# First pair's first five token tiles in float32r pairs beside the conditioning, the residual gate's row in four pieces, and u's loads in another order

## The chip, the core and the metric

The kernel runs on one core of a Trainium2 chip. The metric is the time of one execution on the device in microseconds (us): the median of three runs before the change is 989.02 us (987.64 to 989.61). The core's engines work side by side, each through its own queue in order: TensorE (PE; its weight loads are listed as PEld), VectorE (DVE), ScalarE (ACT), GpSimd (POOL), and SyncE (SP), which here only issues DMA transfers.

## The reference, cut to what matters

One layer works on 1,152 tokens: 1,024 samples (8 tiles of 128) and 128 prompt tokens (tile 8), D_MODEL = 1024, everything in float32.

```python
shift, scale, gate = split(silu(cond) @ w_ada + b_ada, 3)      # conditioning, one row per kind of token
h = rmsnorm(x, norm_g) * (1 + scale) + shift
q, k, v, z_a, u_b, z_b, u_c, z_c, g_a, g_b, g_c = split(h @ w_in)
q = rmsnorm(heads(q), q_g); k = rmsnorm(heads(k), k_g)
y_a = attention(q, k, v)          # window of 8 x 16 and 128 cached keys
y_b = real(fft2(u_b)) @ w_fnet    # Fourier mixing
y_c = pool(u_c) * pool_scale      # centred means over 2, 4, 8, 16 tokens
merged = sigmoid(g_a)*((silu(z_a)*y_a) @ p_a) + sigmoid(g_b)*((silu(z_b)*y_b) @ p_b) + sigmoid(g_c)*((silu(z_c)*y_c) @ p_c)
y = x + gate * (merged @ w_o)     # also returned: k and v of the prompt
```

## The kernel before, in words

Float32 products are made of pairs: an operand is split into a high part and the rest, and `mm3` (lines 163 to 166) issues three matmuls, high by high, high by low and low by high. Pairs are float16 with a power-of-two scale in the projections (`split16`, line 111), and float32r without a scale in the later small products (`two`, `split_r`). A float32r matmul of 384 columns counts as one instruction, as a float16 one does; a plain float32 matmul is two.

**Start (lines 331 to 558, in the order written out by hand, each engine in the order of the program).** The conditioning needs the 8 MB of `w_ada`'s shift and scale parts. `load_wa` brings 16 pieces of 512 KB into 6 buffers; `ada_piece` (line 390) multiplies a piece, two plain float32 matmuls in 32-column groups of the array (`tile_position`), and after every four pieces `ada_row` copies the row out (ACT) and `ada_end` transposes it (PE) and forms a quarter of `gs` and `sh` (DVE). Between them the nine x tiles go through `xnorms` (squares on ACT, root on POOL), `xscale` (DVE) and `x_group` (line 379), in three groups of three: for each of 8 column blocks k three transposes into a PSUM bank and one copy into `xT`. When all of `gs` and `sh` is there, `scale_h` (line 421) finds one bound for h and from it `shs`, the power of two by which h becomes float16. Only then can `make_h` (line 455) split h into `hh` and `hl`, and the first projection begins: `p1_mm` for pair 0 (heads 0 and 1: 384 columns of q, k, v), five token tiles at once, block k by block k, 120 matmuls in five PSUM banks (lines 536 to 558). Among these matmuls lie `make_h` of the next k, `head_scales` (line 476), `v_scales` (line 460) and `new_pair` (line 235), the scales that the heads need. `p1_done` (line 269) finishes a tile (squares, roots, norms, float16 pairs), its parts put off by `later` to certain steps; `tick` counts a step. Pair 0's weights come through `prep` (line 115): four loads, four squares on ACT for a scale, a matmul, and four `split16`.

Then a chain of segments fills PE between the attention's steps. Segment 0 is `p1_tiles` of tiles 8, 5, 6, 7 of pair 0 (line 875); among its steps are `prep` of pair 1, `cached_k` and `cached_v`, at step 21 `group_q` (transposes of q, line 636), at step 24 `group_k` and at step 30 `setup_prompt` (line 670).

**Pooling and Fourier stage (lines 1008 to 1246).** Here a planner orders the instructions. `z_chunk` makes the gates z (three chunks of 24 matmuls for each of four row blocks). The u's, written to DRAM by earlier steps, are loaded one after another behind the small constants (lines 1027 to 1050). `pool_sums` and `pool_diff` (DVE) make the centred means, `pool_out` (line 1085) multiplies them chunk by chunk, `gate_chunk` (line 995) gates a chunk: product on DVE, high part on ACT, low part on POOL. The Fourier products follow (`fold`, `over_channels`, `over_positions`), then the gating of branch b in six chunks.

**Branch projections (lines 1249 to 1419, by hand again).** Sixteen steps n of three chunks (18 matmuls of float32r) project branches c and b; `p_next` splits weights two steps ahead (DVE), `p_chunk` copies a chunk out (ACT) and stores it, with six buffers for chunks under way. Beside it `a_load` and `a_gate` bring branch A's y and z and gate them (steps 0 to 11), and `combos` makes sums for a later stage (DVE and ACT). After every second step `add_wg` (line 1352) adds one of eight pieces of the residual gate's row: for each half n a plain float32 matmul into column group m % 4 of a bank; `load_wg` brings 512 KB per piece, two buffers. Steps 16 to 23 project branch A, and the gated merge and the output projection follow; neither is changed.

Of the kernel before, what the change touches and what calls it, by code (L numbers as in the profile page):

```python
# [35 lines left out]
NWA = 6  # L36
# [3 lines left out]
def mixer_layer(ctx: ExitStack, tc: tile.TileContext, xs, xp, smalls, qgrow, kgrow, bgate, wss, wgate, w1, w3, pw, wo,  # L40
# [74 lines left out]
    def prep(pieces, name):  # L115
# [65 lines left out]
    G.memset(mhalf, -0.5)  # L181

# [12 lines left out]
    with tc.tile_pool(name="hp", bufs=1, side="right") as hp:  # L195
        hh, hl = [], []
        for i in range(2):
            hh.append(hp.tile([P, 4, NT], F16, name=f"hh{i}"))
            hl.append(hp.tile([P, 4, NT], F16, name=f"hl{i}"))
# [28 lines left out]
        with tc.tile_pool(name="qkv", bufs=1) as qkv:  # L228
# [40 lines left out]
            def p1_done(c, t, pt, wait):  # L269
# [61 lines left out]
            with tc.tile_pool(name="st", bufs=1) as st:  # L331
# [12 lines left out]
                def load_x(t):  # L344
                    xt[t] = st.tile([P, D], F32, tag="xt", name=f"xt{t}", bufs=6)
                    nc.sync.dma_start(xt[t], xs[t * P:(t + 1) * P, :] if t < 8 else xp)
# [29 lines left out]
                XG = ((0, 1, 2), (3, 4, 5), (6, 7, 8))  # L376
                xT = st.tile([P, KT, NT], F32, name="xT")

                def x_group(ts):

                    n = len(ts) * P
                    for k in range(KT):
                        pt = bank(("s", "pt", "s")[k % 3], f"xt{k}_{ts[0]}")
                        for i, t in enumerate(ts):
                            T.transpose(pt[:, i * P:(i + 1) * P], xt[t][:, k * P:(k + 1) * P], ident)
                        (V.tensor_copy if k % 2 == 0 else S.copy)(xT[:, k, ts[0] * P:ts[0] * P + n], pt[:, :n])
# [3 lines left out]
                def ada_piece(i):  # L390
                    b, j = divmod(i, 4)
                    if j == 0:
                        pas[b] = bank("p1", f"pa{b}")
# [27 lines left out]
                def scale_h():  # L421
# [5 lines left out]
                    V.scalar_tensor_tensor(ab[:, 3:4], ab[:, 1:2], 31.0, ab[:, 2:3], op0=ALU.mult, op1=ALU.add)  # L427
                    pb = bank("po", "pbd")
# [4 lines left out]
                    V.tensor_scalar(md, ident[:2, :2], m1, None, op0=ALU.mult)  # L433
                    pb2 = bank("po", "pbs")
# [6 lines left out]
                    return hm  # L441

                def v_bound(hm):
# [4 lines left out]
                def h_full(k, eng):  # L448
                    for a, c in ((slice(0, NS), 1), (slice(NS, NT), 0)):
                        if eng is S:  # L450
                            S.activation(xT[:, k, a], xT[:, k, a], AF.Identity, bias=sh[:, k, c:c + 1], scale=gs[:, k, c:c + 1])
                        else:
                            V.tensor_scalar(xT[:, k, a], xT[:, k, a], gs[:, k, c:c + 1], sh[:, k, c:c + 1], op0=ALU.mult, op1=ALU.add)

                def make_h(k):
                    a = slice(0, NT)
                    S.activation(hk(hh, k, a), xT[:, k], AF.Copy, scale=shs)  # L457
                    V.scalar_tensor_tensor(hk(hl, k, a), xT[:, k], shs, hk(hh, k, a), op0=ALU.mult, op1=ALU.subtract)  # L458
# [37 lines left out]
                prep0 = prep_pair(0)  # L496
                wu0 = None
                for what in ("w0", "w1", 0, 1, 2, "w2", "w3", 3, 4, 5, "w4", "w5", "w6", "w7", 6, 7, 8, "w8", "w9", "w10", "w11"):
                    load_x(what) if isinstance(what, int) else load_wa(int(what[1:]))
                run(prep0, 1)  # L500
                for i in range(12, 16):
                    load_wa(i)
# [4 lines left out]
                ada_piece(0)  # L507
                ada_piece(1)
                xnorms(XG[0])
                xscale(XG[0])  # L510
                ada_piece(2)
                ada_piece(3)
                ada_row(0)
                x_group(XG[0])
                ada_end(0)
                xnorms(XG[1])
                xscale(XG[1])
                ada_piece(4)
                ada_piece(5)
                x_group(XG[1])  # L520
                ada_piece(6)
                ada_piece(7)
                ada_row(1)
                xnorms(XG[2])
                ada_end(1)
                ada_piece(8)
                xscale(XG[2])
                x_group(XG[2])
                for i in (9, 10, 11):
                    ada_piece(i)  # L530
                for k in range(4):
                    h_full(k, (S, V)[k % 2])
                ada_row(2)
                ada_end(2)
                run(prep0, 4)
                h_full(4, V)
                h_full(5, V)
                ada_piece(12)
                run(prep0, 1)
                ada_piece(13)  # L540
                run(prep0, 1)
                ada_piece(14)
                run(prep0, 3)
# [9 lines left out]
                for k in range(6):  # L553
# [13 lines left out]
                    if k == 3:  # L567
                        v_scales(vall)
# [1203 lines left out]
```

## Time and profile before

| what | value |
|---|---|
| runs before | 987.64, 989.02, 989.61 us |
| the profiled execution | 992.83 us; span from first to last instruction 990.3 us |
| mean granted TensorE clock | 0.967 |
| busy in the span | PE 922.5, PEld 677.0, DVE 658.8, ACT 489.7, POOL 208.4 us |
| first matmul of pair 0, tile 0 | at 73.89 us |
| first matmul of the branch projections | at 504.96 us |
| moved over the span | 125.02 MB |

The profile is one execution of its own, 3.8 us (0.4%) above the median of the runs. Its page has a strip of 40 slices of 24.8 us: a digit is the busy share of an engine in tenths, PEclk the granted clock in tenths. Rows of the timeline read: start, duration, engine, line, operation, output and inputs, count, and in brackets how long the engine was idle before and what released it. Rows by stretch give for each engine its busy time and, in brackets, its instructions, then the granted clock (1.00 is full), the share of time that the DMA engines were busy, and GB/s. Rows by group give count, total busy us and mean ns of one. SPq is the queue in which SP issues transfers.

### The profile page before, as it was taken

What the parts mean: (1) busy time and instruction counts of PE and PEld (TensorE: products, weight loads), DVE (VectorE), ACT (ScalarE), POOL (GpSimd) and SP (SyncE); (2) the same over time, 40 slices, a digit from 0 to 9 for tenths busy, and PEclk for the clock granted to TensorE, in tenths of its full rate; (3) what the DMA queues carried; (4) which work ended last, traced back from release to release, by engine and by line L of the source; (5) the groups of instructions that cost most, each with busy time, mean ns of one, the idle gap of its engine ahead of it and who ended that gap; (6) DMA issues with size and microseconds to landing.
All of it is one profiled execution on the core that took longest, in us unless ns stands there. A gap on an engine that the chain in (4) does not pass through costs nothing.

```text
span 990.3 us, 17726 instructions
## 1 busy us (share of the span) xinstructions
PE 922.5 (93%) x6554; PEld 677.0 (68%) x6554; DVE 658.8 (67%) x1443; ACT 489.7 (49%) x1017; POOL 208.4 (21%) x352
## 2 busy tenths in 40 slices
PE   4668899999989999998969999999999999999998
PEld 2324566666656666764757779988888888877886
DVE  2347767767767555549767868478989789765322
ACT  3354757757756646644535644545555454442100
POOL 0000765255254332002132200002021020200000
PEclk9568999999999999998988999999999999999999
DMA  7731351251241141250138965453444332228321
GB/s 300 276 107 37 79 152 44 59 170 34 57 131 33 48 149 55 104 188 0 59 104 291 318 237 197 152 176 96 152 126 122 129 105 79 67 71 297 117 75 53
DMA packets 75781, 125.02 MB, mean 126 GB/s; under 512 B 12031, under 2 KB 45227, under 8 KB 75695
## 3 DMA queue, kind: packets, MB, share of 16 engines
q1 hardware_dynamic: 75695, 123.89, 38.8%
q8 instruction: 51, 0.84, 0.3%
q14 instruction: 35, 0.29, 0.1%
HBM read 88.20 MB, written 29.11 MB: 118 GB/s over the span
## 4 chain that ended last, share of the span: by engine, by line
PE 77%; DVE 7%; ACT 5%; DMA 5%; issue 3%; POOL 2%; SPq 1%; ACTq 0%; DVEq 0%; POOLq 0%
PE p L166 3%; PE p L164 3%; PE p L165 3%; PE wo L164 3%; PE wo L166 3%; PE wo L165 3%; PE xc L164 3%; PE xb L164 3%; PE xb L166 3%; PE xc L166 3%; PE xb L165 3%; PE xc L165 3%; PE m L164 3%; PE m L166 3%; PE m L165 3%; PE xa L164 3%
## 5 line engine op out<-in xcount | busy, mean ns | idle before, releaser
L164 PE MATMUL p<-wh_q,hh 128*128 128x384 f16 x288 | 95.3, 331 | 1.9 <-ACT hh L457 1.9
L166 PE MATMUL p<-wh_q,hl 128*128 128x384 f16 x288 | 95.1, 330 | 1.1 <-DVE hl L458 1.1
L165 PE MATMUL p<-wl_q,hh 128*128 128x384 f16 x288 | 95.1, 330 | 0.0
L733 DVE CUSTOM_DVE_ANT_0 sn<-s,bias 128x512 f32<-128x512 f32 x64 | 44.0, 688 | 32.3 <-PE s L729 30.5
L164 PE MATMUL m<-hh,wh_m 128*128 128x384 f16 x192 | 62.6, 326 | 0.0
L166 PE MATMUL m<-hh,wl_m 128*128 128x384 f16 x192 | 62.6, 326 | 0.0
L165 PE MATMUL m<-hl,wh_m 128*128 128x384 f16 x192 | 62.6, 326 | 0.0
L164 PE MATMUL wo<-woh,mh 128*128 128x512 f32 x144 | 56.8, 394 | 1.2 <-ACT woh L1525 1.2
L165 PE MATMUL wo<-wol,mh 128*128 128x512 f32 x144 | 56.6, 393 | 0.0
L166 PE MATMUL wo<-woh,ml 128*128 128x512 f32 x144 | 56.4, 392 | 0.0
L754 ACT CAST pts<-pt 128x512 f16<-128x512 f32 (+1 forms) x72 | 39.7, 552 | 29.4 <-PE pt L752 28.0
L95 POOL TENSOR_SCALAR wsc_g<-wsc_g 128x1 f32<-128x1 f32 x12 | 2.6, 218 | 222.8 <-DVE wsc_g L94 222.8
L758 DVE TENSOR_TENSOR pts<-pt,pts 128x512 f16<-128x512 f32 (+1 forms) x72 | 46.2, 642 | 3.9 <-ACT pts L754 3.2
L744 ACT ACTIVATE sn<-sn,mn 128x512 f32<-128x512 f32 x64 | 46.2, 721 | 3.9 <-DVE mn L733 3.9
L1654 DVE TENSOR_TENSOR yo<-wo,gb 128x512 f32<-128x512 f32 x18 | 12.4, 691 | 50.1 <-PE wo L166 45.9
L777 DVE TENSOR_SCALAR yt<-po,ri,vf 128x64 f32<-128x64 f32 x72 | 24.7, 343 | 29.7 <-PE po L773 26.4
L166 PEld LDWEIGHTS <-hl 128*128 128x128 f16 x288 | 28.5, 99 | 21.0 <-DVE hl L458 1.8
L164 PEld LDWEIGHTS <-hh 128*128 128x128 f16 x288 | 28.8, 100 | 19.0 <-ACT hh L457 2.0
L166 PEld LDWEIGHTS <-wl_m 128*128 128x128 f16 x288 | 28.4, 99 | 19.3 <-issue 1.3
L164 PEld LDWEIGHTS <-wh_m 128*128 128x128 f16 x288 | 29.0, 101 | 17.3 <-issue 1.1
L290 POOL TENSOR_TENSOR rs<-rs,mhalf 128x4 f32<-128x4 f32 x36 | 40.0, 1110 | 3.0
L165 PEld LDWEIGHTS <-wh_m 128*128 128x128 f16 x288 | 28.4, 99 | 17.3 <-issue 1.0
(650 smaller groups left out, 2950.3 us busy)
## 6 DMA issues: line engine op xcount, KB each, us to landing
wa<-in_wss_dram SPq DMA_DIRECT2D x16, 512.0 KB, 6.3
wr_q<-in_w_dram SPq DMA_DIRECT2D x16, 384.0 KB, 4.9
wr_m<-in_w_dram SPq DMA_DIRECT2D x24, 256.0 KB, 3.1
pp_c<-pec SPq DMA_DIRECT2D x24, 192.0 KB, 6.0
pp_b<-peb SPq DMA_DIRECT2D x24, 192.0 KB, 4.9
pp_a<-pea SPq DMA_DIRECT2D x24, 192.0 KB, 1.8
ppxc<-pp_c SPq DMA_DIRECT2D x16, 288.0 KB, 3.9
ppxb<-pp_b SPq DMA_DIRECT2D x16, 288.0 KB, 3.1
```

What stands on the lines that cost most here:

```text
L95: G.tensor_scalar(sc_[:, 2:3], sc_[:, 2:3], 1e-36, None, op0=ALU.max)
L164: T.matmul(out, lh, rh, start=first, stop=False)
L165: T.matmul(out, lh, rl, start=False, stop=False)
L166: T.matmul(out, ll, rh, start=False, stop=last)
L290: G.tensor_tensor(rs, rs, mhalf, op=ALU.pow)
L733: V.tensor_tensor_reduce(out=sn, in0=pS, in1=bt.rearrange("p a b -> p (a b)"), op0=ALU.add, op1=ALU.min, scale=1.0, scalar=3e38, accum_out=mn)
L744: S.activation(e[:, :n], it["sn"], AF.Exp, bias=it["mn"], scale=-1.0, accum_out=sm_)
L754: S.copy(pts[:, 0, :n], pt[:, :n])
L758: V.tensor_tensor(pts[:, 1, :n], it["pt"][:, :n], pts[:, 0, :n], op=ALU.subtract)
L777: V.tensor_scalar(yt[:, hd * 64:hd * 64 + 64], po[:, :64], ri, c["un"], op0=ALU.mult, op1=ALU.mult)
L1654: V.tensor_tensor(yo, pt, gb[0 if t == 8 else 1][:, cols], op=ALU.mult)
```

## The change

Three things change.

1. In the start, tiles 0 to 4 of pair 0 are no longer multiplied from the float16 pairs of h. For each block of two k, `h_early` forms h for 640 tokens (DVE) and splits it into float32r pairs `eh`, `el` (ACT, DVE), `w_split` does the same with a raw weight tile (768 columns), and `block` issues 30 matmuls into the same five banks. Blocks 0 to 2 stand between the pieces of the conditioning, the fourth behind it. x goes through in groups of 2, 3, 2 and 2 tiles. `wa` has 4 buffers in place of 6, x 5 in place of 6, and the order of the loads is another one. The float16 weights, `head_scales`, `v_scales`, `new_pair` and `make_h` now stand behind the fourth block, `make_h` first for tokens 640 to 1151 and, behind the five `p1_done`, for the other 640. For these tiles `p1_done` has scales of its own, and one more product on POOL.
2. In the pooling stage the two u's of branch c are loaded ahead of the small constants, two half copies go from DVE to ACT, memsets from POOL to DVE, the first chunk of branch b's z stands ahead of the second `pool_out`, and the low parts of branch b's gating go from POOL to DVE.
3. The residual gate's row is added after steps 5, 8, 11 and 14, two pieces at a time, for each half both pieces (their column groups differ); the next two pieces are loaded behind that.

```diff
-NWA = 6
+NWA = 4
+NE = 5 * P
...
+            if halves and i == 1:
+                yield unit
+        unit["raws"] = raws
         yield unit
...
+                    if "gi" in c:
+                        G.tensor_scalar(rs, rs, c["gi"], None, op0=ALU.mult)
...
+                def h_part(k, a, c, eng=V):
+                    if eng is S:
+                        S.activation(xT[:, k, a], xT[:, k, a], AF.Identity, bias=sh[:, k, c:c + 1], scale=gs[:, k, c:c + 1])
+                    else:
+                        V.tensor_scalar(xT[:, k, a], xT[:, k, a], gs[:, k, c:c + 1], sh[:, k, c:c + 1], op0=ALU.mult, op1=ALU.add)
+
+                def h_early(ks):
+                    for k in ks:
+                        h_part(k, slice(0, NE), 1)
+                        S.copy(ek(k)[0], xT[:, k, :NE])
+                    for k in ks:
+                        hi, lo = ek(k)
+                        V.tensor_tensor(lo, xT[:, k, :NE], hi.bitcast(F32), op=ALU.subtract)
+
+                def h_late(k, eng):
+                    h_part(k, slice(NE, NS), 1, eng)
+                    h_part(k, slice(NS, NT), 0, eng)
+
+                def w_split(i, raw):
...
+                    S.copy(hi, raw)
+                    V.tensor_tensor(lo, raw, hi.bitcast(F32), op=ALU.subtract)
...
+                def block(b):
+                    for k in (2 * b, 2 * b + 1):
+                        for t in range(early):
+                            p1_r(pts[t], t, k, k == 0, k == KT - 1)
...
+                for what in ("w0", "w1", 0, 1, "w2", "w3", 2, 3, 4, "r", "w4", "w5", "w6", "w7", "r", 5, 6, "w8", "w9", "w10", "w11",
+                             7, 8, "w12", "w13", "w14", "w15"):
...
+                ada(0, 1)
+                norm((0, 1))
+                ada(2, 3)
                 ada_row(0)
+                x_group((0, 1), free)
                 ada_end(0)
+                norm((2, 3, 4))
+                x_group((2, 3, 4), free)
+                w_split(0, raws[0])
+                h_early((0, 1))
+                ada(4, 5, 6, 7)
                 ada_row(1)
+                pts = [bank(ebank[t], f"p1_0_{t}") for t in range(early)]
+                block(0)
                 ada_end(1)
+                w_split(1, raws[1])
+                h_early((2, 3))
+                norm((5, 6))
+                ada(8, 9)
+                block(1)
+                ada(10, 11)
                 ada_row(2)
+                x_group((5, 6), ("po",))
                 ada_end(2)
+                w_split(2, raws[2])
+                h_early((4, 5))
+                norm((7, 8))
+                run(prep0, 5)
+                ada(12, 13)
+                block(2)
+                ada(14, 15)
+                ada_row(3)
                 run(prep0, 1)
+                x_group((7, 8), ("po",))
+                for k in range(6):
+                    h_late(k, (S, V)[k % 2])
+                ada_end(3)
+                w_split(3, raws[3])
+                h_early((6, 7))
                 run(prep0, 1)
+                sc = scale_h()
+                next(sc)
                 for t in range(early):
                     for k in (6, 7):
+                        p1_r(pts[t], t, k, False, k == KT - 1)
+                    if t == 1:
+                        next(sc)
+                    if t == 3:
+                        next(sc, None)
...
+                h_late(6, S)
+                h_late(7, V)
+                wu0 = wu = run(prep0, 4)
+                inverse_of(wu["sc"])
+                head_scales(kall)
+                v_scales(vall)
+                c0 = new_pair(0, wu)
...
+                for k in range(KT):
+                    make_h(k, slice(NE, NT))
+                for t in range(early):
+                    tick()
+                    tick()
+                    p1_done(c0e, t, pts[t], 8)
+                for k in range(KT):
+                    make_h(k, slice(0, NE))
...
+                u_load(0, "c0")
+                u_load(1, "c1")
                 pwt = bp.tile([P, 2], F32, name="pwt")
                 nc.sync.dma_start(pwt, poolw)
...
-                        e.tensor_copy(s4[0:64, 8:UW - 8], s2[0:64, 8:UW - 8])
+                        S.copy(s4[0:64, 8:UW - 8], s2[0:64, 8:UW - 8])
...
-                pool_out(1, *pool_diff(1, f1), zc1)
+                d1 = pool_diff(1, f1)
+                next_z()
+                pool_out(1, *d1, zc1)
...
-                        gate_chunk(zbs[i][:, a], yb[i], th[i], tl[i], a)
+                        gate_chunk(zbs[i][:, a], yb[i], th[i], tl[i], a, V)
...
-                def add_wg(m):
-                    g = 32 * (m % 4)
-                    for n in range(2):
+                def add_wg(ms):
+                    for n, m in [(n, m) for n in range(2) for m in ms]:
+                        g = 32 * (m % 4)
                         T.matmul(gbank[n][g:g + 32], sil[:, m], wgs[m][:, n * 512:(n + 1) * 512], start=(m < 4), stop=(m >= 4),
                                  tile_position=(0, g))
...
-                    if n % 2 == 1:
-                        add_wg(n // 2)
-                        if n // 2 + 2 < 8:
-                            load_wg(n // 2 + 2)
+                    if n in (5, 8, 11, 14):
+                        m = 2 * (n // 3 - 1)
+                        add_wg((m, m + 1))
+                        for m in (m + 2, m + 3):
+                            if m < 8:
+                                load_wg(m)
```

More of the change, by code (lines that the diff above doesn't have):

```diff
@@ L113, in split16, with prep @@
         V.scalar_tensor_tensor(lo, raw, sc_[:, 0:1], hi, op0=ALU.mult, op1=ALU.subtract)
[L115 removed]
+    def prep(pieces, name, halves=False):
         unit = {"w": []}
@@ L181, in mixer_layer @@
     G.memset(mhalf, -0.5)
+    eighth = pers.tile([P, 1], F32, name="eighth")
+    G.memset(eighth, 0.125)
     col = pers.tile([P, 44], F32, name="col")
@@ L193, in mixer_layer @@
     kb_ = pers.tile([P, 8], F32, name="kb_")
-    with tc.tile_pool(name="hp", bufs=1, side="right") as hp:
+    with ExitStack() as hctx:
         hh, hl = [], []
-        for i in range(2):
-            hh.append(hp.tile([P, 4, NT], F16, name=f"hh{i}"))
-            hl.append(hp.tile([P, 4, NT], F16, name=f"hl{i}"))
         def hk(z, k, a):
@@ L455, in make_h, with ek @@
[L455 to L458, printed above, removed]
+                ectx = ExitStack()
+                ep = ectx.enter_context(tc.tile_pool(name="ep", bufs=1, side="right", reuse_waits="tile"))
+                ets = {}
+                def ek(k):
+                    if k not in ets:
+                        ets[k] = [ep.tile([P, NE], F32R, tag=x, name=f"{x}{k}", bufs=6) for x in ("eh", "el")]
+                    return ets[k]
@@ new lines, in p1_r @@
+                def p1_r(pt, t, k, first, last):
+                    eh, el = ek(k)
+                    a = slice(t * P, (t + 1) * P)
+                    b = slice((k % 2) * CH, (k % 2) * CH + CH)
+                    hi, lo = wr_[k // 2]
+                    mm3(pt[:, :CH], eh[:, a], el[:, a], hi[:, b], lo[:, b], first, last)
+                def block(b):
+                    for k in (2 * b, 2 * b + 1):
+                        for t in range(early):
+                            p1_r(pts[t], t, k, k == 0, k == KT - 1)
@@ L494, in head_scales @@
                     V.tensor_copy(kb_, pks[:, :8])
[L496 to L502, printed above, removed]
+                prep0 = prep([w1[0, i] for i in range(4)], "q0", True)
+                for what in ("w0", "w1", 0, 1, "w2", "w3", 2, 3, 4, "r", "w4", "w5", "w6", "w7", "r", 5, 6, "w8", "w9", "w10", "w11",
+                             7, 8, "w12", "w13", "w14", "w15"):
+                    if isinstance(what, int):
+                        load_x(what)
+                    elif what == "r":
+                        r0 = run(prep0, 1)
+                    else:
+                        load_wa(int(what[1:]))
+                raws = r0["raws"]
                 kall = st.tile([64, 4, 2, P], F32, tag="wa", name="kall", bufs=NWA)
@@ new lines, in mixer_layer @@
+                for i in range(2):
+                    hh.append(hp.tile([P, 4, NT], F16, name=f"hh{i}"))
+                    hl.append(hp.tile([P, 4, NT], F16, name=f"hl{i}"))
+                h_late(6, S)
[5 more added lines that the diff above has]
+                c0 = new_pair(0, wu)
+                gi = pers.tile([P, 1], F32, name="gi")
+                V.reciprocal(gi, wu["inv"])
```

155 lines of the change are left out of this document (57 added, 98 removed).

## The prediction

> **What bounds the kernel now.** I read the strip of the page first, then the stretches, then the groups of the start, then the timeline and the waits of the stages that the diff touches.
>
> ```profile
> PE   4668899999989999998969999999999999999998
> PEclk9568999999999999998988999999999999999999
> ```
>
> Only the first three slices (some 74 us), the slice of 495 to 520 and a few with an 8 hold time in which PE is not busy; everywhere else the kernel goes at PE's pace. So a change can win in the start, or at single stalls of PE. By stretch (PE, PEld, DVE, ACT, POOL, granted clock, DMA share, GB/s):
>
> ```profile
> 40.60:44.00 3.40, 2.04 (x12) 1.11 (x12) 0.56 (x4) 3.27 (x6) 0.00 (x0) 0.97 0.68 223
> 44.00:57.70 13.70, 9.28 (x36) 4.93 (x36) 6.27 (x11) 4.49 (x9) 1.11 (x2) 0.51 0.16 60
> 97.70:121.80 24.10, 20.11 (x132) 11.94 (x130) 17.62 (x48) 17.39 (x39) 16.77 (x25) 1.00 0.34 87
> 455.00:460.50 5.50, 5.50 (x19) 2.81 (x20) 5.37 (x7) 2.01 (x5) 3.29 (x3) 0.53 0.00 0
> 511.40:582.00 70.60, 61.85 (x286) 47.13 (x284) 52.45 (x107) 38.67 (x88) 14.78 (x13) 0.93 0.91 298
> 540.00:560.00 20.00, 20.00 (x96) 15.50 (x95) 16.99 (x35) 12.43 (x28) 5.67 (x5) 1.00 0.99 335
> ```
>
> Three things are to be seen. In the conditioning the clock is mostly half (0.51). Behind the first matmuls DVE is busy 17.62 of 24.10: it has 6.5 us to spare there and no more. In the branch projections the DMA engines are busy 0.91 of the stage, 0.99 in its middle.
>
> **Part A, the start.** The change moves 120 matmuls from behind `shs` to between the pieces of the conditioning. PE, ACT and DVE each go through the new order as written, so I walk through it. The rows for the durations, timeline and then groups:
>
> ```profile
> 25.64 1.94 PE L398 MATMUL pa<-wa,sil 128*32 128x512 f32 x8
> ...
> 37.21 1.54 PE L385 MATMUL xt<-ident,xt 128*128 128x128 f32 x6 [0.57 <-ACT xT L386]
> ...
> 42.29 1.05 PE L398 MATMUL pa<-wa,sil 128*32 128x512 f32 x4
> ...
> 67.98 1.05 PE L410 MATMUL pb<-pick,ar 128*128 128x2 f32 x8 [0.69 <-ACT ar L404]
> ...
> 73.89 0.50 PE L164 MATMUL p<-wh_q,hh 128*128 128x384 f16 x1 [1.93 <-ACT hh L457]
> ...
> 100.90 0.33 PE L164 MATMUL p<-wh_q,hh 128*128 128x384 f16 x1
> ...
> 510.04 0.34 PE L165 MATMUL ppc<-tl,oh_p 128*128 128x384 f32 x1
> ...
> 510.56 0.33 PE L165 MATMUL ppc<-tl,oh_p 128*128 128x384 f32 x1
> ...
> 524.35 0.52 PE L165 MATMUL ppb<-tl,oh_p 128*128 128x384 f32 x1
> 524.67 0.52 PE L166 MATMUL ppb<-th,ol_p 128*128 128x384 f32 x1
> ```
>
> ```profile
> L458 DVE SCALAR_TENSOR_TENSOR hl<-xT,shs,hh 128x1152 f16<-128x1152 f32 x8 | 11.0, 1408 | 0.0
> L366 ACT ACTIVATE xsq<-xt 128x1024 bf16<-128x1024 f32 x9 | 9.5, 1057 | 7.7 <-DMA xt<-in_xs_dram 7.5
> ...
> L113 DVE SCALAR_TENSOR_TENSOR wl_q<-wr_q,wsc_q,wh_q 128x768 f16<-128x768 f32 x8 | 8.0, 1018 | 2.6 <-ACT wh_q L112 2.6
> L86 ACT ACTIVATE wjk_q<-wr_q 128x768 bf16<-128x768 f32 x8 | 6.7, 843 | 0.1
> ...
> L453 DVE TENSOR_SCALAR xT<-xT,gs,sh 128x1024 f32<-128x1024 f32 x5 | 4.0, 807 | 0.0
> L451 ACT ACTIVATE xT<-xT,sh,gs 128x1024 f32<-128x1024 f32 x3 | 3.7, 1232 | 0.0
> ```
>
> A float32r matmul of 384 columns is 0.173 at the full clock (three in 0.52 between the 510 rows) and 0.32 at half (the 524 rows). A block of 30 is thus 5.2 or 9.7. No row shows the new splits; taken from the nearest groups (estimates): high copy of 768 weights on ACT 0.84 (L86), low part on DVE 0.95 (just under L113), h for 640 tokens 0.6 (L453, 0.81 for 1024), high copy of it 0.7 (L86 in proportion, 640 of 768).
>
> Block 0: today's second group of x is transposed by 38.75 (row 37.21); the first group now has two tiles instead of three, so eight transposes (0.26 each by that row), a square and a scale fewer stand ahead: I put it at 34.0. Then 0.5 for the last copy out, 0.84 + 0.95 + 0.6 + 0.7 and 0.4 for four hand-overs: the block starts at 38.0. As the clock now turns full at 40.60 behind a busy stretch and falls back at 44.00, I let it run at half to 44: 46.1. Block 1: transposes of the row 1.0 (L410 row), small DVE work 0.75, then 0.95 + 0.6 + 0.7: 50.1 to 57.3, part of it at half. Then the pieces 10 and 11 (1.0, the 42.29 row), transposes of x5, x6 2.7, the row's 1.1; DVE and ACT need 3.6 more, to 65.7. Now ACT has two squares of x (1.18 each) and four of weights (0.84 + 0.19 read-out) ahead of a matmul that PE has next in its order: PE waits until 72.1, a stall of 10 that the trace of before has not. That matmul 0.6 and pieces 12 and 13 1.9 (25.64 row): block 2 runs 74.6 to 81.4. Pieces 14, 15, last transposes and copies: 85.65; three late h on ACT (1.07 each, from L451) 88.9; the splits again 3.1: block 3 from 92.05. Its 30 matmuls are 5.2, the clock's ramp 2.4, and the two small matmuls of the bound with hand-overs 1.7: it ends at 101.3.
>
> So the 120 matmuls end where they end today (100.90 is tile 8's first). They have only changed places with the conditioning: `shs`, written at 72.39 below, comes at about 100.9. What was hidden under them now isn't:
>
> ```profile
> 72.39 0.15 DVE L90 TENSOR_SCALAR shs<-shs 128x1 int32<-128x1 int32 x1
> ...
> 81.22 1.19 DVE L479 TENSOR_REDUCE km<-kall 64x8 f32<-64x1024 f32 x1
> ...
> 85.86 0.21 DVE L484 TENSOR_REDUCE gm<-pkm 8x1 f32<-8x64 f32 x1 [3.33 <-PE pkm L483]
> ...
> 87.42 0.11 DVE L494 COPY kb__91<-pks 128x8 f32<-128x8 f32 x1
> 88.78 0.68 DVE L463 TENSOR_REDUCE vm<-vall 128x4 f32<-128x512 f32 x1
> ...
> 91.24 0.16 DVE L474 COPY vrec<-pvs 128x4 f32<-128x4 f32 x1 [0.47 <-PE pvs L473]
> ...
> 95.31 0.22 DVE L242 TENSOR_SCALAR gs<-qs__89,wsc_q 128x2 f32<-128x2 f32 x1
> ...
> 97.26 0.16 DVE L253 RECIPROCAL vf<-vf 128x1 f32<-128x1 f32 x1
> ...
> 121.83 0.40 PE L674 MATMUL pqp<-id,tok 128*128 128x128 f16 x4 [0.88 <-DVE tok L305]
> ```
>
> On DVE, in order, stand ahead of the first low part of h: bound of v 0.4, h of k = 7 0.7, four weights' low parts 3.9 (L113), inverse 0.35, `head_scales` 3.3 (81.22 to 87.53, less 3.0 of the 3.33 spent behind queued matmuls), `v_scales` 2.6 (88.78 to 91.40), `new_pair` 2.1 (95.31 to 97.42), `gi` 0.2: 13.6. Tile 8 needs the low part, so PE has nothing to do until 114.5: 13.4 later than today. Then DVE must make low parts for 512 tokens (8 at 0.65) and for 640 (8 at 0.78, from L458), 11.4 us that today lie under the 120 matmuls, and its old work of 17.6 (97.70 row). From 114.5 that gives 143.5 for the prompt's q transposes (pqp), at 121.83 today. What PE does there is in order, so the lag is carried on: **A = +22**. Bounds: +13 if all of the DVE backlog hides, +28 if the lag of `shs` (28.4) is passed on whole.
>
> On cover: the loads in another order I cost at nothing, as the trace waits for them only before the first x; if four buffers of `wa` in place of six hold a load up, it is paid ahead of a block, and lies inside +28. POOL's extra product (5 small ones) lies beside DVE's backlog.
>
> **Part B, the pooling stage.**
>
> ```profile
> 429.01 0.38 SPq L1028 DMA_DIRECT2D pwt<-in_poolw_dram  x1
> ...
> 433.91 0.47 SPq L1048 DMA_DIRECT2D uc<-u_d  x1
> ...
> 439.82 1.39 DVE L1058 TENSOR_TENSOR s<-uc 128x1183 f32<-128x1183 f32 x1 [3.64 <-DMA uc<-u_d]
> ...
> 454.79 0.69 PE L164 MATMUL yc<-dh,wph 128*128 128x384 f32 x1 [4.44 <-ACT yc L1091]
> ```
>
> The first load of u goes from 433.91 to the place of 429.01, 4.9 earlier, so DVE's wait of 3.64 goes; two half copies leave DVE (0.76 each, half of the 1.39 row and its fixed part). PE's stall of 4.44 behind the chain of sums should go, and with it the half clock of 455.00 to 460.50 (0.53, so 2.75 of 5.5 lost): at most 7.2. The chunk of z put ahead of the second `pool_out` covers what stays. Low parts of branch b go to DVE, which has room where nothing waits on it. The small constants come later, and the pooling weights are first used behind the sums. **B = -6**, between -2 (the ACT copies of half sums, which ACT must fit in, take the stall's place) and -7.2.
>
> **Part C, the branch projections.**
>
> ```profile
> 520.34 3.59 PE L1355 MATMUL gr<-wg,sil 128*32 128x512 f32 x4 [8.75 <-DMA wg<-in_wgate_dram]
> ...
> 580.67 1.90 PE L1355 MATMUL gr<-wg,sil 128*32 128x512 f32 x4
> ```
>
> ```profile
> ACT pec L1278 <- DMA pp_c<-pec: 5.9, 5, 1.9
> ```
>
> On PE the change removes the wait of 8.75 (the first pair comes four steps later), half clock behind it, 2.35 (520.3 to 525 at 0.50), and for each pair of pieces one call: four matmuls in one column group take 1.90 (580.67), eight in different groups 1.94 (25.64), so 4 x 1.84 = 7.35. Sum -18.4. But the stage moved 298 GB/s x 70.6 us = 21.0 MB, and the change moves the same. At the 335 GB/s of 540 to 560, with the engines 0.99 busy, that takes 62.8, 7.8 less than now; the six chunks of stores under way at the end (6 x 197 KB, 3.5 us) needn't have landed, and I take half of that: **C = -10**. ACT waits already for the stores of a chunk (5.9 in all) and would wait more. Ends -8 and -18. By the Trainium skill, "DMA: Bandwidth & Descriptors", section "Where 436 GB/s comes from", the memory side gives a core some 358 GB/s: then the stage would be 58.7 and C about -14; the measured 335 at 0.99 busy decides here.
>
> Sum: 22 - 6 - 10 = +6. The profiled execution took 992.83 (span 990.3), 3.8 above the median; I carry the difference over to the median: 989.0 + 6 = **995**. About 0.2% (2 us) is what a measurement of this kernel can tell from no change.
>
> **Rivals.**
> *The clock stays full in the start* (faster). The blocks make PE denser; the clock decides in each stretch of 3.4 us. If it is full from 30 us on, transposes save 2.5, block 0 2.4, block 1 1.6, block 2 with its pieces 2.5 and block 3 2.4: 11.5, so A = +11 and the time is 984. It decides from 6 us recovered on. Against it: the clock fell at 44.00 though the last matmuls had ended at 43.34 (row 42.29). The Trainium skill, "TensorE: Matmul & The Clock Gate", section "Why this matters for your kernels", has it fall only after an idle gap of some 3 us; the fall after 0.66 us does not agree. Chance 0.18.
> *PE, not DMA, paces the branch projections*: C = -18, 987. For it speaks that the early waits for wg leave DMA unused in places (0.91 against 0.99); against it the 0.99. Chance 0.14.
> *DVE's backlog behind `shs` hides*: A = +13, 986. For it the 6.5 us that DVE has to spare; against it that 11.4 don't fit in 6.5. Chance 0.08.
> *The stalls of B come back elsewhere, or `shs` is passed on whole*: A + 6 or B and C 7 less, 1002. Chance 0.12.
>
> **How the numbers follow.** The forecast has 0.48, with 990 to 1003 as its own range. Slower by over 0.2%: 0.44 of it, 0.12 of the last rival, 0.02 of the others: 0.58. Faster: 0.15 of the clock, 0.08 of PE's pace, 0.06 of the backlog: 0.29. Within: 0.13. The range reaches down to the clock's case and up over the last: 982 to 1003.
>
> **What would show it.** In the changed profile `shs` stands near 100 (72.39 now), the four blocks start near 38, 50, 75 and 92, PE waits some 10 us for the weight squares before block 2 and 13 before tile 8, and pqp stands near 143. The yc wait of 4.44 and the wg wait of 8.75 are gone; the branch projections last some 60 us with DMA at 0.99 and longer waits of pec for its stores. The prediction is wrong if the blocks run at the full clock from the first, if `shs` comes before 92, if PE doesn't stand still ahead of tile 8, or if the DMA share in the branch projections falls as they get shorter.

## The result, and the profile after

The changed kernel takes 1001.31 us (median of 4 runs, 1000.55 to 1005.22), the kernel before 988.33 (986.64 to 989.61): a ratio of 1.0135, 95% interval 1.011 to 1.016. That is 13.0 us slower, where 6 was forecast. The profiled execution took 1001.46, its span is 999.4; it stands at the median of its runs, whereas that of before stood 4.5 above its own (992.83 against 988.33), so the spans of the two traces differ by only 9.1 (999.4 against 990.3).

The strip of the page after, for the two rows that were shown of before:

```profile
PE   3865389999999989999898999999999999999998
PEclk8777689999999999999999999999999999999999
```

The fifth slice (100 to 125 us) is a 3 in which before had an 8: PE stands still there. The start is read from its timeline (PE first, then DVE; the columns are those of before):

```profile
35.12 0.44 PE L168 MATMUL p<-wrh,eh 128*128 128x384 f32 x1 [1.59 <-ACT eh L476]
...
44.76 0.44 PE L168 MATMUL p<-wrh,eh 128*128 128x384 f32 x1 [1.89 <-ACT eh L476]
...
66.59 0.56 PE L134 MATMUL pw_q<-wss_q,onesp 128*128 128x4 f32 x2 [9.51 <-issue]
...
68.95 0.69 PE L168 MATMUL p<-wrh,eh 128*128 128x384 f32 x1
...
86.46 0.69 PE L168 MATMUL p<-wrh,eh 128*128 128x384 f32 x1 [5.45 <-ACT eh L476]
...
107.55 0.50 PE L170 MATMUL p<-wh_q,hl 128*128 128x384 f16 x1 [2.24 <-DVE hl L487]
127.61 0.59 PE L134 MATMUL pw_q<-wss_q,onesp 128*128 128x4 f32 x2 [12.54 <-ACT wjk_q L87]
...
141.24 0.40 PE L739 MATMUL pqp<-id,tok 128*128 128x128 f16 x4 [0.88 <-DVE tok L310]
```

```profile
93.40 0.15 DVE L91 TENSOR_SCALAR shs<-shs 128x1 int32<-128x1 int32 x1
...
94.55 3.80 DVE L114 SCALAR_TENSOR_TENSOR wl_q<-wr_q,wsc_q,wh_q 128x768 f16<-128x768 f32 x4
...
98.53 1.19 DVE L529 TENSOR_REDUCE km<-kall 64x8 f32<-64x1024 f32 x1
...
106.76 5.37 DVE L487 SCALAR_TENSOR_TENSOR hl<-xT,shs,hh 128x512 f16<-128x512 f32 x8
...
115.38 6.84 DVE L487 SCALAR_TENSOR_TENSOR hl<-xT,shs,hh 128x640 f16<-128x640 f32 x8
```

In these rows `p<-wrh,eh` is a product of the new float32r pairs, `pw_q` the small matmul over the squares of a pair's weights, and `pqp` the transposes of the prompt's q. The four rows with an `eh` are the first matmuls of the four blocks, at 35.1, 44.8, 69.0 and 86.5. Ahead of block 2 PE stands still for 9.51 at the small matmul over the squares of the first pair's weights; the row names no releaser, but ACT ends the last of these squares at 66.50, just ahead of the matmul's 66.59. `shs` comes at 93.55, 21 later than before. From there DVE works 13.2 through its chain (93.55 to 106.76) until the first low part of h, and PE's first matmul with one stands at 107.55. Behind it is a stall of 12.54: PE's queue is held by the small matmul over the squares of the second pair's weights, and ACT, which makes these squares, has the high parts of h for the first five tiles and what waits for DVE ahead of them. In the kernel before the same matmul waited 0.43:

```profile
107.83 0.39 PE L130 MATMUL pw_q<-wss_q,onesp 128*128 128x4 f32 x2 [0.43 <-ACT wjk_q L86]
```

The matmul comes 19.8 later than before, and the prompt's q transposes (pqp) 19.4. Of these, 6.65 were lost by the first low part of tile 8 (107.55 for 100.90), the rest behind it. By stretch (the last two rows are the branch projections, whole and their middle 60 us):

```profile
35.10:41.00 5.90, 5.64 (x32) 5.32 (x32) 1.55 (x2) 1.80 (x3) 0.00 (x0) 1.00 1.02 409
...
68.90:76.10 7.20, 7.20 (x37) 6.90 (x34) 0.00 (x0) 0.00 (x0) 0.00 (x0) 0.73 0.66 182
86.40:94.00 7.60, 7.54 (x33) 6.72 (x33) 3.45 (x15) 5.38 (x9) 0.00 (x0) 0.78 0.00 0
93.60:107.50 13.90, 3.19 (x12) 1.58 (x10) 11.32 (x40) 6.05 (x12) 0.00 (x0) 0.61 0.17 57
106.80:141.20 34.40, 19.28 (x109) 10.91 (x109) 29.14 (x65) 22.67 (x47) 21.05 (x30) 0.75 0.27 76
518.60:592.80 74.20, 66.67 (x324) 53.02 (x324) 58.32 (x120) 40.82 (x97) 13.28 (x12) 0.98 0.88 291
523.00:583.00 60.00, 54.89 (x274) 45.12 (x272) 50.14 (x102) 32.55 (x77) 13.28 (x12) 0.97 0.93 303
```

The first three are blocks 0, 2 and 3. While the chain runs, PE is busy 3.19 of 13.90; in the 34.4 behind it DVE is busy 29.14 and PE 19.28. The branch projections are 74.2 long, where before had 79.2 (504.96 to 584.2):

```profile
504.96:584.20 79.24, 70.49 (x324) 53.45 (x324) 59.50 (x114) 42.62 (x97) 20.65 (x18) 0.94 0.83 273
```

PE's waits in the pooling stage and the branch projections, each with what ended it (total, times, longest):

```profile
PE gr L1429 <- DMA wg<-in_wgate_dram: 2.9, 5, 1.3
PE ppc L168 <- DVE oh_p L73: 2.7, 3, 1.7
PE yc L168 <- ACT dh L1152: 2.0, 1, 2.0
...
PE gb L1493 <- ACT gro L1491: 1.1, 1, 1.1
...
PE yc L168 <- ACT yc L1162: 0.9, 1, 0.9
PE ppb L168 <- ACT pec L1352: 0.7, 1, 0.7
```

The single waits of 8.75 (wg) and 4.44 (yc) are gone; in their place stand many small ones. Before, PE was idle for 8.75 of the 79.24, nearly all of it in that one wait. Now it is busy for 66.67 of 74.2 us: the 7.5 that are left nearly make up the 8.75 again.

### The profile page after: what moved, and what is told of

Read it like the earlier page. It is cut to its first block, busy times and chain, and to the rows that moved or that the text cites. A ratio compares the mean times of both kernels' runs of the same rounds, so it can differ in the third digit from the quotient of the medians.

```text
span 999.4 us, 17773 instructions
## 1 busy us (share of the span) xinstructions
PE 911.6 (91%) x6554; PEld 686.0 (69%) x6554; DVE 668.9 (67%) x1478; ACT 498.2 (50%) x1039; POOL 207.2 (21%) x348
## 4 chain that ended last, share of the span: by engine, by line
PE 73%; DVE 10%; DMA 6%; ACT 5%; issue 3%; POOL 2%; SPq 1%; DVEq 0%; POOLq 0%; ACTq 0%
PE p L170 3%; PE p L168 3%; PE p L169 3%; PE wo L168 3%; PE wo L170 3%; PE wo L169 3%; PE xc L168 3%; PE xb L168 3%; PE xc L170 3%; PE xb L169 3%; PE xc L169 3%; PE xb L170 3%; PE m L168 3%; PE m L170 3%; PE m L169 3%
## 5 line engine op out<-in xcount | busy, mean ns | idle before, releaser
L170 PE MATMUL p<-wh_q,hl 128*128 128x384 f16 x248 | 81.9, 330 | 2.2 <-DVE hl L487 2.2
L168 PE MATMUL p<-wh_q,hh 128*128 128x384 f16 x248 | 82.2, 331 | 0.0
L169 PE MATMUL p<-wl_q,hh 128*128 128x384 f16 x248 | 82.1, 331 | 0.0
L1730 DVE TENSOR_TENSOR yo<-wo,gb 128x512 f32<-128x512 f32 x18 | 12.4, 691 | 51.2 <-PE wo L170 51.2
L817 PE MATMUL pt<-ident,sn 128*128 128x128 f32 x256 | 38.5, 273 | 0.0
L170 PEld LDWEIGHTS <-hl 128*128 128x128 f16 x248 | 24.5, 99 | 19.6 <-DVE hl L487 3.1
```

What stands on the lines that cost most here:

```text
L168: T.matmul(out, lh, rh, start=first, stop=False)
L169: T.matmul(out, lh, rl, start=False, stop=False)
L170: T.matmul(out, ll, rh, start=False, stop=last)
L817: T.transpose(pt[:, j * P:(j + 1) * P], it["e"][:, j * P:(j + 1) * P], ident)
L1730: V.tensor_tensor(yo, pt, gb[0 if t == 8 else 1][:, cols], op=ALU.mult)
```

## The experiments

All kernels are timed beside the kernel before; A, B and C are the three parts as the prediction names them. What each did:

| run | median (runs), us | before beside it | ratio, 95% interval |
|---|---|---|---|
| e1_bc | 982.38 (6) | 989.62 | 0.9923 (0.9894 to 0.9953) |
| e2_a | 1007.70 (6) | 989.62 | 1.0178 (1.0147 to 1.0208) |
| e3_c | 989.58 (12) | 989.62 | 0.9993 (0.9973 to 1.0013) |
| e4_before | 992.75 (1) | 989.62 | no interval |
| e5_chain | 996.69 (4) | 988.81 | 1.0074 (1.0047 to 1.0102) |
| e6_squares | 995.78 (6) | 988.81 | 1.0073 (1.0046 to 1.0099) |
| e7_b | 985.62 (12) | 988.81 | 0.9961 (0.9946 to 0.9977) |
| e8_wg | 977.81 (4) | 988.81 | 0.9890 (0.9866 to 0.9914) |
| e9_all | 990.45 (10) | 989.60 | 1.0017 (0.9988 to 1.0046) |
| e10_low | 986.86 (12) | 989.60 | 0.9978 (0.9959 to 0.9996) |
| e11_wgpool | 975.23 (4) | 989.60 | 0.9874 (0.9831 to 0.9918) |
| e12_two | 993.08 (10) | 987.26 | 1.0056 (1.0039 to 1.0074) |

e8_wg and e11_wgpool leave out six of the eight loads of the gate's weights, so their gate row is another one. The runs of the kernel before spread from 983.5 to 994.2 over all of this, so single profiles differ by a few us. For that reason the tables below give stage lengths from several traces.

**The parts alone.** e1_bc is the kernel before with parts B and C of the diff, e2_a with part A, e3_c with part C, e7_b with part B; e4_before is the kernel before, profiled once more.

> The start of the kernel before, with parts B (pooling stage) and C (gate's row) of the change. By the landmarks of the two traces A costs 19.5, B gives 5.8 and C 5.1. If the parts are independent (theory), this kernel takes 988.3 - 10.9 = 977 us, ratio 0.989. Rival: B and C gain only because the longer start shifts what they collide with, then 983 or more. The prediction's own C of 10 would give 972.

> Part A alone (the new start), pooling stage and gate's row as before. Theory: 988.3 + 19.5 = 1008 us, with the q transposes of the prompt at 141 (121.8 before). If the median of the changed kernel (13.0 over that of before, where the traces differ by 9.1) holds 4 us that the traces miss in the start, then 1012.

> Part C alone. Theory from the changed trace: PE's stall of 8.75 becomes many small ones, since the DMA engines move the same 21 MB: 983 us (5 less). The prediction said 978 (10 less); PE pacing the stage would give 970 (18 less); no gain at all would show that the changed trace's 5 came from elsewhere.

> The kernel before itself, for a second profile: the profiled execution shown took 992.83, 3.8 over the median. If that is in the start (clock steps falling otherwise), the first matmul of pair 0 or the q transposes of the prompt come up to 4 us earlier than 73.9 and 121.8 here; if it lies in the branch projections, that stage is shorter than 79.2.

> Part B alone. If B's gain lies in the pooling stage alone, as the prediction has it, 6 less than before: 983. B and C together gave 7.3, C alone nothing: if B makes all of that, 982. If the two need each other (low parts on DVE let SP's loads for the branch projections start earlier, which pays only with the gate's row in four pieces), B alone gives 4 and the branch projections stay at 78: 985.

A alone costs 1.78%, 17.6 us; B alone gives 3.9 parts in a thousand, 3.8 us; C alone gives nothing that can be told from zero. 17.6 - 3.8 - 0.7 = 13.1, where the whole change cost 13.0; so close a match is in part luck, since each term is uncertain by 2 to 3. B and C together give 7.6, more than the 4.5 of the two singly (17.6 - 7.6 would leave 10.0), but the intervals (2.9 either way for the pair) don't separate these. Against what was expected, e2_a came out as put (1008); e7_b took the time of its last case (985), though its branch projections are 75.3 long and not 78; e1_bc lies nearer its rival (983) than the theory (977), and e3_c missed: 983 was expected of C, and there was no gain. e1_bc is faster than both kernels of this case, and the fastest of those that load all eight pieces of the gate's row. e4_before's profile has the same length as the first (span 990.1 against 990.3) with the same stalls. So the profile shown is no odd one, and both profiled executions of this kernel lie in the upper part of its runs; why they do stays open.

The branch projections, from the first ppc matmul to the first ppa matmul, by trace:

| traces | length, us |
|---|---|
| neither B nor C: before, e4_before, e2_a | 79.2, 78.1, 77.4 |
| C alone: e3_c | 76.3 |
| B alone: e7_b | 75.3 |
| low parts of B alone: e10_low | 74.3 |
| B and C: e1_bc, after | 72.7, 74.2 |
| B and C, another start (further down): e5_chain, e6_squares, e9_all, e12_two | 75.0, 72.9, 75.5, 74.6 |
| B and C, six wg loads less: e8_wg, e11_wgpool | 67.9, 68.2 |

Traces of the same code in this stage differ by up to 2.8. B, which was costed in the pooling stage alone, takes some 3 from this stage; C on top of it takes 1 or so (the six with both lie at 74.2 in the mean), which that spread doesn't tell from nothing. The next run shows what B does here.

**One piece of B.** e10_low is the kernel before with a single edit (`gate_chunk` takes the engine as an argument, V is DVE):

```diff
-                        gate_chunk(zbs[i][:, a], yb[i], th[i], tl[i], a)
+                        gate_chunk(zbs[i][:, a], yb[i], th[i], tl[i], a, V)
```

> The kernel before, with one piece of part B alone: the low parts of branch b's gating on DVE instead of POOL. Theory: they end earlier, SP's wait for them (5.7) shrinks, and the loads of the branch projections start earlier in the stage: 3 of B's gain come from here, 986. Rival: the gain of B lies in the u's alone, then 989.

It gives 2.2 parts in a thousand (0.4 to 4.1), by the middle values more than half of B's 3.9; the intervals are too wide for a firm share. The queue's waits in it (of the kernel before the same wait was on POOL and took 5.7):

```profile
SPq L1365 <- DVE tl L999: 3.8, 1, 3.8
```

```profile
510.26 0.33 SPq L1365 DMA_DIRECT2D ya<-yT_d  x1
```

The first load behind the wait is issued 4.4 after the stage's first matmul (505.88 in this trace) instead of 6.3, and the wait for wg shrinks with it, from 8.7 to 4.6:

```profile
PE gr L1355 <- DMA wg<-in_wgate_dram: 4.6, 1, 4.6
```

**What paces the branch projections.** e8_wg is e1_bc with the loads of pieces 2 to 7 of the gate's row left out:

```diff
                             if m < 8:
-                                load_wg(m)
+                                wgs[m] = wgs[m - 2]
```

> Parts B and C on the start of before, but only the first two of the eight pieces of the residual gate's weights are loaded, and used four times: 3.1 MB of the 21 MB of the branch projections are left out, so the gate's row is another one. If the DMA engines pace that stage (theory), it falls from 72.7 by up to 10 (3.1 MB at 305 GB/s), to PE's own 63 to 65: 973. Rival (the order of loads and stores in SP's queue, and the small waits on them, pace it): it stays above 70, 980.

e11_wgpool is e8_wg with the high copy in `split_r` on POOL (G) in place of DVE (V):

```diff
-        V.tensor_copy(hi[:, :n], raw)
+        G.tensor_copy(hi[:, :n], raw)
```

> The kernel with two of the eight pieces of the gate's weights loaded (its gate row is another one), and the high copies of the projection weights' split on POOL instead of DVE. With fewer bytes DVE was busy 46.4 of 50 in the middle of the branch projections. If DVE is what paces the stage there (theory), taking 0.28 x 2 per step from it shortens the stage from 67.9 to 65 or less: 975. Rival (single small waits, or POOL slower in the place of DVE): 978 or more.

The middle 60 us of the stage in e1_bc and then in e8_wg:

```profile
505.00:565.00 60.00, 53.43 (x272) 43.19 (x272) 48.62 (x100) 32.87 (x78) 13.36 (x12) 1.00 0.95 312
```

```profile
507.00:567.00 60.00, 55.09 (x293) 45.95 (x291) 52.67 (x107) 36.67 (x87) 13.61 (x12) 1.00 0.88 285
```

With 3.1 MB less the stage is 4.8 shorter (72.7 to 67.9; against all six traces with B and C, 4.8 to 7.6) and the DMA share falls from 0.95 to 0.88. So the six loads do cost the stage time, though at 305 GB/s their bytes would have given 10: below 68 something else ends last. The run took the loads' bytes away together with their places in SP's queue and PE's waits for them (2.6 in e1_bc), so it doesn't show how much of the 4.8 is owed to the bytes. What PE still waits for in e8_wg:

```profile
PE ppc L164 <- DVE oh_p L72: 2.7, 3, 1.6
PE gb L1428 <- ACT gro L1426: 1.4, 1, 1.4
PE ppb L164 <- ACT pec L1287: 1.0, 1, 1.0
PE ppb L164 <- ACT peb L1287: 0.6, 1, 0.6
PE ppb L164 <- DVE oh_p L72: 0.4, 1, 0.4
```

These add to 6.1, so PE alone would need some 62. e11_wgpool was to show whether DVE, next to PE the busiest engine there (52.67 of 60), is behind them. Its stage is no shorter (68.2). The waits for `oh_p` (2.7 and 0.4) are gone, but waits for ACT's copies of a chunk (2.1 and 1.1 where e8_wg had 0.6 and 1.0) and some time at a lower clock (0.85 granted in 517 to 527) stand in their place. Nor was DVE relieved by much: over the stage it was busy 57.1 after 58.9, since other operations of it took longer in this trace (those of line 1304, in `combos`, 579 ns in place of 449). So moving this copy did not pay in the stage, but the run doesn't settle whether DVE's load matters. That the median came out at the expected 975 is no proof of the theory: the 2.6 between the medians lies ahead of the stage in the traces (it begins at 497.7 and 501.8). Which of the split weights, the copies out and the stores paces the stage below 68 stays open.

**Where the start loses.** The next four are the changed kernel with another order in the start. e5_chain puts the weights' float16 split and the maxima of the k and v ahead:

```diff
                 block(2)
+                wu0 = wu = run(prep0, 6)
+                km, vm = maxima(kall, vall)
                 ada(14, 15)
...
-                wu0 = wu = run(prep0, 4)
...
```

> The changed kernel, but the float16 split of pair 0's weights and the maxima of k and v (DVE 3.8 + 1.2 + 0.67 = 5.7, ACT 3.4) are moved from behind the fourth block into the time of block 2, in which the changed trace has DVE idle from 67.3 to 77.8. Theory (what the new start costs is DVE's chain that lay under the matmuls before): the first low part of h, at 106.8, comes 5.7 earlier, the q transposes of the prompt too (141.2 to 135.5), and the time falls from 1001.3 to 996. Rival (the first pair's stage behind is paced by ACT or by the second pair's weights): the low part comes earlier, the transposes and the time don't.

e6_squares:

```diff
-                run(prep0, 5)
+                run(prep0, 4)
                 ada(12, 13)
                 block(2)
+                run(prep0, 1)
```

> The changed kernel, but the small matmul over the squares of pair 0's weights stands on PE behind block 2 instead of ahead of pieces 12 and 13; the squares stay in ACT's order. Theory: the stall of 9.5 ahead of block 2 (57.1 to 66.6 in the changed trace) shrinks to about 2, until the h of block 2 is split, and shs comes some 7 earlier: 994. Rival (a later wait takes its place, on x's last squares and scales): less than 3, 999 or more.

e12_two moves two of the four blocks back behind the bound:

```diff
                 ada(12, 13)
-                block(2)
                 ada(14, 15)
...
                 ada_end(3)
+                run(prep0, 1)
+                for _ in scale_h():
+                    pass
+                block(2)
                 w_split(3, raws[3])
                 h_early((6, 7))
...
+                wu0 = wu = run(prep0, 4)
...
```

> The changed kernel, but only blocks 0 and 1 stand between the pieces of the conditioning; blocks 2 and 3 come behind the bound of h, and the float16 split of the weights lies under block 3. Theory (a block placed ahead of the bound delays it by its own length and its stalls, and DVE's chain needs matmuls to lie under): shs comes near 79 in place of 93.4, the first matmul with tile 8's low part near 95 in place of 107.5, the time is near 990. Rival (it doesn't matter where the blocks stand, since DVE's whole work behind the conditioning is the same): 997 or more.

e9_all has e5_chain's and e6_squares' edits and forms the late h behind block 3:

```diff
-                for k in range(6):
-                    h_late(k, (S, V)[k % 2])
                 ada_end(3)
...
-                h_late(6, S)
-                h_late(7, V)
+                for k in range(KT):
+                    h_late(k, S)
```

> The changed kernel with both repairs of the start at once (weights' float16 split and maxima beside block 2; the small matmul over the weights' squares behind block 2), and h of the tokens 640 to 1151 formed behind block 3's splits instead of ahead of them. Singly the first two gave 4.6 and 5.5, and the h's are 3.1 of ACT ahead of block 3: if they add, 1001.3 - 13.2 = 988, no slower than before. Rival: ACT, with eight late h's (8.2) behind block 3, becomes late for the high parts of h, and the sum is 3 to 5 less: 992.

The first low part of h in e5_chain, in e6_squares and in e12_two, one fence each:

```profile
99.11 5.37 DVE L487 SCALAR_TENSOR_TENSOR hl<-xT,shs,hh 128x512 f16<-128x512 f32 x8
```

```profile
83.87 0.15 DVE L91 TENSOR_SCALAR shs<-shs 128x1 int32<-128x1 int32 x1
...
97.24 5.37 DVE L487 SCALAR_TENSOR_TENSOR hl<-xT,shs,hh 128x512 f16<-128x512 f32 x8
```

```profile
80.23 0.15 DVE L91 TENSOR_SCALAR shs<-shs 128x1 int32<-128x1 int32 x1
...
98.71 5.38 DVE L487 SCALAR_TENSOR_TENSOR hl<-xT,shs,hh 128x512 f16<-128x512 f32 x8
```

And the q transposes of the prompt in e5_chain and in e6_squares:

```profile
133.69 0.40 PE L741 MATMUL pqp<-id,tok 128*128 128x128 f16 x4 [0.68 <-DVE tok L310]
```

```profile
131.71 0.40 PE L740 MATMUL pqp<-id,tok 128*128 128x128 f16 x4 [0.87 <-DVE tok L310]
```

e5_chain and e6_squares answer to their theories. With 5.7 less on DVE the low part comes 7.65 earlier (some 1.1 of it because `shs` itself is 1.1 earlier in this trace), the transposes 7.55, and the median falls by 4.6. With the stall of 9.5 gone from PE's order, `shs` and the transposes come 9.5 earlier and the median falls by 5.5. The rivals, that a later wait would take their place, fall as far as the transposes: what is taken out ahead of the low part of h arrives there whole. At the end of the program the traces are 4.4 (e5_chain) and 9.3 (e6_squares) shorter, and by the ratios to the kernel before both gain 6, with some 3 us of uncertainty on each. The stall ahead of the second pair's small matmul stays: it is 11.09 in e5_chain, 12.03 in e6_squares, 11.43 in e12_two and 11.88 in e9_all. No run moved that matmul, so what it costs by itself is not shown.

e12_two brings `shs` to 80.4 as expected, but DVE still has 18 us between it and the low part (the splits for blocks 2 and 3 now lie there too), so that comes at 98.7 and not at 95; the time falls by 0.8% of before, to 993. e9_all, expected at 988, reaches 990.45, not measurably slower than before; its interval of 2.9 either way covers the expected time as well as the rival's 992. In the trace the gains don't add: the transposes come 12.4 earlier (128.8), where the first two edits alone had given 7.55 and 9.5. The rival's reason isn't seen there: ACT begins the high parts of h at 88.85, 0.5 after `shs` (88.36). ACT and then PE in its trace, one fence each:

```profile
68.70 2.57 ACT L113 ACTIVATE wh_q<-wr_q,wsc_q 128x768 f16<-128x768 f32 x3
71.17 0.56 ACT L414 COPY ar<-pa 128x512 f32<-128x512 f32 x1
```

```profile
71.79 1.05 PE L393 MATMUL xt<-ident,xt 128*128 128x128 f32 x4 [3.75 <-ACT ar L414]
```

The weights' split had its cover in the 9.5 in which PE stood still ahead of block 2. Without that stall it stands ahead of the copy of the conditioning's last row, PE waits 3.75 for that, and block 3 begins at 80.48, where e6_squares had it at 76.04. No order of the new start that was run is faster than the old one with the same B and C (982.4).

## Why the prediction was wrong

The direction was right, and so was the mechanism of part A, but the size was not: +13 against +6. By its steps:

**The step that failed is C = -10.** What failed is the pace set by the DMA engines, 335 GB/s from the first load on, and with it that the wait of 8.75 would be won. C alone measured 0.7 (between 2.7 less and 1.3 more), and 3.8 on top of B (e7_b against e1_bc, some 3 either way). The DMA engines moved 303 to 312 GB/s over the middle 60 us at a share of 0.93 to 0.95, not 335 at 0.99: the 335 was the best 20 us of the stage, taken as its pace. From the first load to the stage's end the changed kernel took 69.8 at 305 GB/s, where 61 to 63 was reckoned. (By the 358 GB/s of the Trainium skill, "DMA: Bandwidth & Descriptors", section "Where 436 GB/s comes from", C would have been overestimated further, though the loads of the start, at 409, went above that figure.) And the loads begin 4.4 to 6.3 after the stage's first matmul, since SP's queue waits for the low parts of branch b; C doesn't touch that. The stall of 8.75 was spread, not removed: in e3_c, which has C alone, PE is idle for 8.7 of the stage's 76.3 in pieces of at most 3.3. That the transfers are behind all of these small waits is argued; what the runs show is that six loads less shorten the stage by 4.8, and that PE stays idle for some 6 even then.

PE's own saving by C was right for a pair of pieces that has landed, but by luck. The 1.94 was read at 25.64, where the granted clock was 0.50 and the eight matmuls lay in four column groups; at the full clock such eight take 1.06. The gate's eight lie in two groups a bank and take 1.91 at the full clock. And only the first of the four pairs ran so: ahead of the others PE waited for the second piece, and they took 2.95 busy:

```profile
25.64:27.58 1.94, 1.94 (x9) 0.20 (x8) 0.56 (x4) 1.88 (x5) 0.00 (x0) 0.50 0.94 376
```

```profile
41.81 1.06 PE L408 MATMUL pa<-wa,sil 128*32 128x512 f32 x8
...
544.30 1.91 PE L1429 MATMUL gr<-wg,sil 128*32 128x512 f32 x8
...
556.27 1.04 PE L1429 MATMUL gr<-wg,sil 128*32 128x512 f32 x2 [0.49 <-DMA wg<-in_wgate_dram]
557.49 1.90 PE L1429 MATMUL gr<-wg,sil 128*32 128x512 f32 x6 [0.18 <-DMA wg<-in_wgate_dram]
```

The first fence is of the kernel before, the second of the changed one.

**B = -6** measured 3.8 (2.3 to 5.3), at the low side of its range but inside it. The yc wait went from 4.44 to 2.9 in two pieces, so not all of it went; how much the copies on ACT and the moved chunk of z each did was not tested. By the middle values over half of what B gives (2.2 of 3.9) came from where it had been costed at nothing, the low parts on DVE, through SP's queue in the next stage.

**A = +22** measured 17.6 (14.5 to 20.6), 19.4 in the traces. The walk held up to `shs`: the four starts were foreseen at 38, 50, 75 and 92 and stand at 35, 45, 69 and 86.5; the stall ahead of the weights' small matmul is 9.5 for 10, DVE's chain 13.2 for 13.6, pqp 141 for 143.5. `shs` was put too late (100.9, measured 93.55), for three reasons: block 0 began 2.9 earlier; it went at the full clock throughout (its stretch shows 1.00, 5.9 long, where 8.1 was put), which is the first rival's mechanism in its first block only; and from the start of block 3 to `shs` it was 7.1 for 8.85. The ramp in block 2 was near what was put (7.2 long for 6.8, 0.73 granted). What `shs` came early, 7.4, was mostly lost behind it: tile 8's first low part was foreseen for 114.5 and came at 107.55, but pqp gained only 2.3 on the forecast. So the forecast had split its 22 otherwise than the trace: it put 13.6 ahead of tile 8 and 8 behind it, the trace has 6.7 and 12.8. The part behind was too small, since the second pair's squares in ACT's order, and PE's stall of 12.54 on them, are not in the forecast. That A came out as near as it did is owed in part to two errors of opposite sign.

**The sum.** The three terms alone add to 13.1. The error of 7 is C (9.3 too much) and B (2.2 too much), less 4.4 by which A was put too high. Carrying the profile's 3.8 over to the median made no error by itself, but between the two profiles the change costs 9.1 only.

Of the rivals, PE as the pace of the branch projections (C = -18) fell: without the bytes of six loads the stage still didn't reach it. That DVE's backlog behind `shs` hides fell: DVE was busy 29.14 of 34.40 while PE waited. The last rival (1002), in its form that B and C give 7 less, came nearest, with its place in C; that its number is hit within 1 us is luck, since B and C singly gave 11.5 less and A cost 4.4 less. The signs that were named for a wrong prediction did not come, but for block 0's full clock: `shs` was not before 92, PE stood still ahead of tile 8, and the DMA share rose. What was wrong, the pace of the stage, shows in two of the things that were expected to be seen: the length (some 60 us; 69.8 from the first load) and the share of 0.99 (0.93 in the middle). Of what else was foreseen there, ACT's longer waits for a chunk's stores did come (pec waited 5.9 before and 9.5 after).

## What to carry to other kernels

A transfer rate taken from the busiest stretch of a stage is a bound, not a pace: use the stage's mean, and look at what holds the first load of the stage in its queue. When work is moved ahead of the step that everything waits for, count the chain of other engines that used to lie under it; here it came out into the open at nearly its full length (13.2 us). A small matmul for a side chain holds PE's whole queue until its input is there (9.5 and 12.5 us here), so ask when that input will come. A stall that disappears on one engine is won only if the sum of that engine's small waits doesn't grow; read the busy time of the whole stage, not the one row.

## What the hardware showed that was not expected

The clock, in two stretches of the changed trace:

```profile
30.20:33.60 3.40, 3.33 (x23) 1.38 (x21) 1.35 (x3) 1.69 (x3) 0.00 (x0) 0.77 0.00 0
33.70:37.10 3.40, 1.74 (x8) 1.42 (x9) 2.68 (x5) 2.57 (x4) 0.00 (x0) 1.00 0.93 331
```

Behind transposes and pieces of the conditioning PE had 1.00 from 33.7 on, and kept it through the 1.59 idle ahead of block 0 (row 35.12), whereas in the kernel before it went back to half by 44.00, at most 0.66 after the last matmul had ended. The gap of some 3 us that the Trainium skill names ("TensorE: Matmul & The Clock Gate", section "Why this matters for your kernels") agrees with the first and not with the second. The second is seen only in the granted clock, as no matmul ran there until 46.88. But a fall after a short gap is seen in the matmuls too: in the changed kernel PE was idle for 1.89 ahead of block 1 (row 44.76), the granted clock fell to half by 45.5, and the block's matmuls from 46.11 on took 0.52 in place of 0.33. Which rule the clock follows here, these runs don't show.

The DMA engines at a share of 1.02 moved 409 GB/s in 35.1 to 41.0, in the start, where there are loads and no stores; at 0.93 to 0.99 in the branch projections, with loads and stores mixed, they moved 303 to 335. For each full share that is 401 GB/s in the start and 326 to 338 in the branch projections, so the busy share doesn't give the rate. The start's transfers are also larger (512 KB, where the stage has 128 to 512 KB); whether size or the mix makes the difference was not tested.
